# w_down of the second group in seven products over pairs of steps, with the weight sums made beside the projection

## The chip, the cores and the metric

The kernel runs on one core of a Trainium2 chip. What counts is the device time of one execution in microseconds. Before the change it is 2610.94 us, the median of three runs between 2605.71 and 2612.57 us. One more execution was recorded by the profiler; its own time is in the table below.

## What is computed

One layer of a hybrid decoder, for a prompt of 2048 tokens and 8 samples of 4 tokens, in float32:

```python
xn = rms_norm(x, norm_mix_pre)
qk_raw, v_m, o_m, gates, q_a, k_a, v_a = split_projection(xn @ w_in)
...                                    # mLSTM heads: y_m; sliding-window heads with sinks: y_a
mix = concatenate([y_m, y_a], axis=-1) @ w_out                 # 1024 x 1024
x = x + rms_norm(mix, norm_mix_post)
u = rms_norm(x, norm_ffn_pre)
f = square(relu(u @ w_up)) @ w_down                            # 1024 x 4096, 4096 x 1024
x = x + rms_norm(f, norm_ffn_post)
x = x + sigmoid(x @ w_pgate) * (p @ w_pproj)
```

The outputs are x for the prompt and the samples, and the states of both kinds of heads.

## The kernel before

**Precision.** Each float32 matrix is split into a high part, rounded to the type that TensorE multiplies at full rate, and a low part, the rest. `mm3` makes a product of three matmuls (high by high, high by low, low by high), so every product below counts three matmuls at line 148.

**Stages.** The prompt is 16 blocks of 128 tokens, in six chunks of three or two blocks. First the projection runs over all six chunks (`project`), with the mLSTM, the attention and the decoding of the samples beside it. Then three groups of two chunks follow (blocks 0 to 5, 6 to 11, 12 to 15 with the samples): w_out, the MLP and the gate. In the names of the trace `mo` is a result of w_out, `up` of w_up, `dn` of w_down, `pg` of the gate; `f` holds the sums of w_down and `hh`, `hl` are the parts of the squared activations.

**The MLP.** It has 16 steps of two tiles of 128 hidden columns each. Steps 0 and 1 are plain. In steps 2 to 15 w_up is done for both chunks together with seven block products in place of eight (`up_both`; the sums of the activations are made once for a group, those of the weights in the ring). w_down is plain in all steps: two halves of 512 output columns, two chunks, three blocks, two tiles and three passes, 72 matmuls a step in a group of six blocks. Each block's result stands in one of three banks of the pool `ps_mm` and VectorE adds it to `f` (L1759). w_up's results have two banks of their own (`ps_s`), added by VectorE at L1734.

**Weights.** `Ring` brings all weights in the order that `plan()` gives. A weight that comes first is loaded raw through SyncE's queue into one of five raw buffers (`RAWS`; L351, L363), copied to its high part by ScalarE (L254), and its low part is subtracted by VectorE and GpSimd in turn (L255). The two parts stand in one of seven pair buffers (`PAIRS`). A weight that is needed again is stored to DRAM as a split pair by GpSimd's queue (L282, `wk<-w` in the trace) and loaded from there the next time by SyncE's (L289, `w<-wk`).

**Order.** TensorE's instructions are pinned in the order in which the program writes them. Work beside the main line comes from generators, called sides, that are asked for their next piece between products after so many microseconds of estimated TensorE time; `pe.drain` empties one. The other engines' instructions are placed by a scheduler, except those marked with `here`, which keep their program order. Each engine works through its instructions in order, and so does each queue of DMA issues (SyncE's and GpSimd's). A buffer of a pool goes to the next tile that asks for it, and the first write into it waits until the last reader of the old tile is done.

The part of the main program where the projection ends:

```python
    for ci, blocks in enumerate(CHUNKS):
        project(ci, blocks)
    pe.drain(swa)
...
    es_proj.close()
    es0.close()
```

## Time and profile before

| | |
|---|---|
| profiled execution, its own time | 2623.78 us |
| its span in the trace | 2621.7 us |
| mean granted TensorE clock | 0.989 |
| chain that ended last: TensorE's share | 77%, of which w_up 21%, w_down 21%, w_out 5%, the gate 5% |
| w_down's matmuls, high part of the activations (`dn<-w,hh`) | 1792, 564.0 us busy |
| w_down's matmuls, low part (`dn<-w,hl`) | 896, 354.5 us busy |
| VectorE's additions of w_down's results (L1759) | 420, 286.9 us busy |
| transfers over the whole span | 651.10 MB, 248 GB/s on average |

The time of the execution is the span and some two microseconds around it. An engine's busy time is the sum of its instructions' times. Matmul records overlap, so that their busy times by group add up to more than the time on the clock; the pace of TensorE is better read from the chain, whose pieces follow each other. In the views below "x" stands for a number of instructions, "out<-in" for the tiles an instruction writes and reads, and what follows "<-" in brackets behind an idle time is what ended it.

### The profile page before, as it was taken

The page shows a single profiled execution, that of the slowest core. Times are in us where ns is not written, and L with a number is a line of the kernel's source. Part 1 is how long each engine was busy: PE and PEld are TensorE (multiplying, and loading weights), DVE is VectorE, ACT ScalarE, POOL GpSimd, SP SyncE. Part 2 cuts the span into 40 slices and gives each one's busy share as a digit, 9 for nine tenths or more (in the row PEclk, how much of TensorE's full clock was granted, in tenths as well). Part 3 has the DMA queues.
Part 4 walks back from the last instruction along what each step waited for, and adds up shares of the span by engine and source line. Part 5 has one row for each costly group of instructions (what it writes and reads, how often), then busy time and mean ns, then how long its engine had stood idle before and what let it go on. Part 6 is the DMA issues. An engine that isn't in the chain of part 4 may idle for free.

```text
span 2621.7 us, 39337 instructions
## 1 busy us (share of the span) xinstructions
PE 2534.7 (97%) x14260; PEld 2204.3 (84%) x14260; DVE 1483.0 (57%) x3162; ACT 974.3 (37%) x2167; POOL 620.3 (24%) x988
## 2 busy tenths in 40 slices
PE   7999999998999999999999999999999999999998
PEld 7787888777778888888877788999998879999986
DVE  6666656665657655656744654444446346444553
ACT  5545444544445444444523342222223134222231
POOL 5311111112433666666523200000001011000010
PEclk9999999999999999999999999999999999999999
DMA  9756656576898666666799765555556899777787
GB/s 315 273 192 201 207 181 213 194 244 227 260 343 287 254 250 253 244 254 251 271 341 318 255 201 188 188 191 188 187 187 233 295 334 359 253 255 256 256 299 235
DMA packets 220433, 651.10 MB, mean 248 GB/s; under 512 B 25397, under 2 KB 59401, under 8 KB 220224
## 3 DMA queue, kind: packets, MB, share of 16 engines
q1 hardware_dynamic: 170032, 474.02, 53.4%
q0 software_dynamic: 50160, 174.54, 17.3%
q8 instruction: 113, 1.85, 0.3%
q14 instruction: 80, 0.66, 0.1%
q10 hardware_dynamic: 48, 0.03, 0.0%
HBM read 494.34 MB, written 155.25 MB: 248 GB/s over the span
## 4 chain that ended last, share of the span: by engine, by line
PE 77%; DVE 8%; DMA 7%; issue 3%; ACT 2%; POOL 2%; SPq 0%; ACTq 0%; DVEq 0%; POOLq 0%
PE up L148 21%; PE dn L148 21%; PE mo L148 5%; PE pg L148 5%; PE v L148 3%; DMA w<-wk 3%; PE o L148 3%; DMA wk<-w 2%; PE qk L148 2%; PE qa L148 2%; PE gv L148 2%; DVE hl L232 2%; PE aT L152 1%; PE aO L148 1%; PE pv L148 1%
## 5 line engine op out<-in xcount | busy, mean ns | idle before, releaser
L148 PE MATMUL dn<-w,hh 128*128 128x512 f32 x1792 | 564.0, 396 | 6.3 <-ACT re L1654 3.8
L1759 DVE TENSOR_TENSOR f<-f,dn 128x512 f32<-128x512 f32 x420 | 286.9, 686 | 220.5 <-PE dn L148 218.4
L148 PEld LDWEIGHTS dn<-w,hh 128*128 128x128 f32 x1792 | 334.2, 189 | 84.7 <-DVE f L1759 6.8
L148 PE MATMUL dn<-w,hl 128*128 128x512 f32 x896 | 354.5, 396 | 1.6 <-DVE hl L232 1.6
L1734 DVE TENSOR_TENSOR re<-up,re 128x384 f32<-128x384 f32 (+1 forms) x294 | 151.9, 517 | 320.2 <-PE up L148 320.2
L148 PEld LDWEIGHTS dn<-w,hl 128*128 128x128 f32 x896 | 168.8, 188 | 43.5 <-DVE hl L232 5.1
L1735 ACT COPY re<-up 128x384 f32<-128x384 f32 (+1 forms) x42 | 18.8, 448 | 392.0 <-PE up L148 392.0
L1654 ACT ACTIVATE re<-re 128x384 f32<-128x384 f32 (+1 forms) x168 | 83.0, 494 | 207.5 <-DVE re L1734 203.9
L232 DVE TENSOR_TENSOR hl<-re,hh 128x384 fp32r<-128x384 f32 (+1 forms) x192 | 137.6, 717 | 16.8 <-ACT hh L231 15.7
L282 POOL DMA_DIRECT2D wk<-w x242 | 134.1, 556 | 34.4 <-DVE w L255 25.2
L254 ACT CAST w<-wr 128x512 fp32r<-128x512 f32 (+2 forms) x152 | 88.9, 597 | 95.9 <-PE up L148 32.3
L254 ACT CAST w<-wb 128x512 fp32r<-128x512 f32 x98 | 60.6, 620 | 168.4 <-PE dn L148 114.6
L255 POOL TENSOR_TENSOR w<-wr,w 128x512 fp32r<-128x512 f32 (+2 forms) x76 | 100.2, 1319 | 80.5 <-ACT w L254 79.5
L255 POOL TENSOR_TENSOR w<-wb,w 128x512 fp32r<-128x512 f32 x70 | 92.3, 1319 | 110.3 <-ACT w L254 109.8
L1460 POOL DMA_DIRECT2D x<-x1d x16 | 8.7, 545 | 463.5 <-PE up L148 449.4
L1655 ACT ACTIVATE re<-re 128x384 f32<-128x384 f32 (+1 forms) x192 | 94.9, 494 | 5.9
L231 ACT CAST hh<-re 128x384 fp32r<-128x384 f32 (+1 forms) x192 | 92.6, 482 | 8.3
L1067 ACT ACTIVATE s<-s,swt 128x257 f32<-128x257 f32 (+1 forms) x128 | 63.3, 496 | 65.8 <-DVE swt L1064 65.8
L1061 DVE CUSTOM_DVE_ANT_0 s<-aS,cst,sink 128x256 f32<-128x256 f32 (+1 forms) x128 | 57.1, 472 | 52.0 <-PE aS L148 51.6
L148 PE MATMUL up<-t2h,w 128*128 128x384 f32 (+1 forms) x336 | 85.1, 320 | 0.0
L148 PE MATMUL up<-t0h,w 128*128 128x384 f32 (+1 forms) x336 | 85.1, 320 | 0.0
L148 PE MATMUL up<-t1h,w 128*128 128x384 f32 (+1 forms) x336 | 85.1, 320 | 0.0
(1526 smaller groups left out, 6415.7 us busy)
## 6 DMA issues: line engine op xcount, KB each, us to landing
w<-wk SPq DMA_DIRECT2D x728, 512.0 KB, 4.9
wk<-w POOLq DMA_DIRECT2D x238, 512.0 KB, 7.2
wr<-in_w_down_dram SPq DMA_DIRECT2D x64, 256.0 KB, 8.2
wb<-in_w_up_dram SPq DMA_DIRECT2D x28, 512.0 KB, 6.9
w<-wk SPq DMA_DIRECT2D x20, 528.0 KB, 3.9
x<-in_x_prompt_dram SPq DMA_DIRECT2D x16, 512.0 KB, 4.4
y<-yd SPq DMA_DIRECT2D x32, 256.0 KB, 7.0
xr<-in_x_prompt_dram POOLq DMA_DIRECT2D x16, 512.0 KB, 9.4
```

The source lines that it names most:

```text
L148: ins = self.pe.matmul(out, lhsT, rhs, start=start, stop=stop)
L231: act.copy(hi, src)
L232: dve.tensor_tensor(lo, src, hi.bitcast(F32), ALU.subtract)
L254: act.copy(hi, src)
L255: ins = (eng or weng()).tensor_tensor(lo, src, hi.bitcast(F32), ALU.subtract)
L282: here(put(self.kept[key], t.bitcast(U32)))
L1061: dve.tensor_tensor_reduce(s_[:, s, lo : 2 * P], pS[:, s, lo:], bias[:, j, lo:], 1.0 if s == 0 else 0.0625, sink[:, h : h + 1], ALU.add, A ...
L1067: act.activation(e_, e_, AF.Exp, bias=nm[:, s : s + 1], accum_out=sm[:, s : s + 1])
L1654: act.activation(t, src, AF.Relu)
L1655: act.square(t, t)
L1734: add = lambda out, a, b: dve.tensor_tensor(out, a, b, ALU.add)
L1759: dve.tensor_tensor(out(i), out(i), ps, ALU.add)
```

## The change

In steps 2 to 13 of the second group (`SEVEN`, `SGROUP`) w_down is done over pairs of steps with seven block products instead of eight. Rows of the two by two scheme are the two chunks, its columns the two hidden tiles of a step, and the columns of the result are the two halves of w_down's output. Both steps of a pair are accumulated in the same bank.

- `up_seven` takes the place of `up_both`: it makes the four blocks of activations and four sums of them, s1 to s4, and splits each (`parts`), on VectorE (L1754 and L1723 of the kernel after the change) and GpSimd.
- `down_seven` does the seven products of a pair in the order A12, A11, s3, A22, s1, s4, s2. Three of them go to two sums each; two products go to a common sum U, which `share` adds to nine blocks on GpSimd after step 13. The gain of the last norm, `gffn`, is loaded after that, since U takes its buffer.
- The sums of w_down's blocks, four of them for each of the twelve steps, are made beside the projection by the new side `prep`, from the second chunk on (`differences`): four loads by GpSimd's queue into raw buffers of the ring, four subtractions on VectorE, four stores to DRAM by GpSimd's queue. They are emptied out (`pe.drain(prep)`) at the projection's end. `Ring.diff` loads such a sum later like a raw weight and splits it with GpSimd.
- `rows_seven` puts the weights of a pair in the plan in the order of the products.
- The pool `sp2` has one buffer instead of two, and the pool `wide` is closed in the second group before step 2, where `hq`, `wq` and `us` take its place.

```diff
+SEVEN = range(2, STEPS - 2)
+SGROUP = 1
+DIFW = 16.0, 4.0, 8.0
...
-    swa, mls, tsp = pe.side(), pe.side(), pe.side()
+    swa, mls, tsp, prep = [pe.side() for _ in range(4)]
...
+        def diff(self, key, src):
+            def make(h, l):
+                raw = self.load(512)
+                dma(raw, src)
+                wsplit(h, l, raw, pool)
+            return self.get(key, 512, make)
...
+        def diff(s, i):
+            return ("t", s, i), lambda key: ring.diff(key, td[s, i])
+        def rows_seven(steps):
+            for i, k, half in ((0, 1, 0), (0, 0, 0), (3, 0, 0), (4, 0, 0), (1, 0, 0), (0, 1, 1), (2, 0, 0)):
+                for s in steps:
+                    yield diff(s, i) if i else row(w_down, s * FS + k, half)
...
             for s in range(FAST, STEPS):
...
-                yield from rows_down(s)
+                if gi == SGROUP and s in SEVEN:
+                    if s % 2:
+                        yield from rows_seven((s - 1, s))
+                else:
+                    yield from rows_down(s)
...
+    td = {(s, i): dram.tile([P, 512], F32, name=f"td{s}{i}") for s in SEVEN for i in range(1, 5)}
     ring.set_plan(plan())
+    def differences():
+        sub = lambda out, a, b: here(dve.tensor_tensor(out, a, b, ALU.subtract))
+        for s in SEVEN:
+            b11, b21, b12, b22 = b = [ring.load(512) for _ in range(4)]
+            for n, t in enumerate(b):
+                k = s * FS + n % 2
+                here(put(t, w_down[k * P : (k + 1) * P, n // 2 * 512 : n // 2 * 512 + 512]))
+            yield DIFW[0]
+            for i, out, x, y in ((1, b11, b12, b11), (3, b12, b22, b12), (2, b22, b22, b11), (4, b21, b21, b22)):
+                sub(out, x, y)
+                yield DIFW[1]
+            for i, out in ((1, b11), (3, b12), (2, b22), (4, b21)):
+                here(put(td[s, i], out))
+            yield DIFW[2]
...
     for ci, blocks in enumerate(CHUNKS):
+        if ci == 1:
+            prep.add(differences())
         project(ci, blocks)
     pe.drain(swa)
+    pe.drain(prep)
...
-    sp2 = es2.enter_context(tc.tile_pool(name="sp2", bufs=2, reuse_waits="tile"))
+    sp2 = es2.enter_context(tc.tile_pool(name="sp2", bufs=1, reuse_waits="tile"))
...
-        gffn = gain(A["norm_ffn_post"], f"gffn{gi}")
...
+        if gi != SGROUP:
+            gffn = gain(A["norm_ffn_post"], f"gffn{gi}")
...
+        def rectify(t):
+            act.activation(t, t, AF.Relu)
+            act.square(t, t)
+        def two_tiles(pool_, nm):
+            return [pool_.tile([P, UW], F32R, tag=f"h{e}", name=f"h{e}{nm}") for e in "hl"]
+        def parts(pool_, t, nm, eng, to=None):
+            h, l = [y[:, : t.shape[1]] for y in to or two_tiles(pool_, nm)]
+            act.copy(h, t)
+            eng.tensor_tensor(l, t, h.bitcast(F32), ALU.subtract)
+            return h, l
+        def up_seven(s, X, hq, wq):
+            W = X[0][0].shape[2]
+            nm = f"{G}{s}"
+            product = products(s, X)
+            A = {}
+            t = [wp.tile([P, UW], F32, tag="re", name=f"re{nm}{n}")[:, :W] for n in range(4)]
+            s1 = wq.tile([P, UW], F32, tag="s1", name=f"s1{nm}")[:, :W]
+            add = lambda out, a, b: dve.tensor_tensor(out, a, b, ALU.add)
+            act.copy(t[0], product(1))
+            add(t[1], product(2), t[0])
+            rectify(t[1])
+            a12, a11 = two_tiles(hp, f"{nm}a12"), two_tiles(hp, f"{nm}a11")
+            A["11"] = parts(hp, t[1], f"{nm}a11", dve, a11)
+            add(t[0], product(6), t[0])
+            add(t[2], product(7), t[0])
+            add(t[3], product(4), t[2])
+            rectify(t[3])
+            A["12"] = parts(hp, t[3], f"{nm}a12", dve, a12)
+            ps = product(5)
+            add(t[2], ps, t[2])
+            add(t[0], ps, t[0])
+            rectify(t[2])
+            A["22"] = parts(hp, t[2], f"{nm}a22", dve)
+            add(t[0], product(3), t[0])
+            rectify(t[0])
+            pool.tensor_tensor(s1, t[0], t[2], ALU.add)
+            dve.tensor_tensor(t[0], t[1], t[0], ALU.subtract)
+            A["s3"] = parts(hq, t[0], f"{nm}s3", dve)
+            A["s1"] = parts(hq, s1, f"{nm}s1", pool)
+            pool.tensor_tensor(t[1], s1, t[1], ALU.subtract)
+            pool.tensor_tensor(t[3], t[3], t[1], ALU.subtract)
+            A["s4"] = parts(hp if s % 2 else hq, t[3], f"{nm}s4", pool)
+            A["s2"] = parts(hp if s % 2 else hq, t[1], f"{nm}s2", pool)
+            return A
+        def down_seven(s, As, U, first):
+            c0, c1 = chunks
+            def out(ci, half):
+                return lambda i: f[chunks[ci][i]][:, half * 512 : half * 512 + 512]
+            u = lambda i: U[i]
+            uses = (
+                ("12", out(0, 0)),
+                ("11", u, out(0, 0)),
+                ("s3", out(1, 1), out(1, 0)),
+                ("22", out(1, 0)),
+                ("s1", out(1, 1), out(0, 1)),
+                ("s4", out(0, 1)),
+                ("s2", u),
+            )
+            for n, (a, *to) in enumerate(uses):
+                w = [[t[:, :512] for t in w] for w in ring.take(2)]
+                for i in range(len(c0)):
+                    ps = psum(ps_mm, f"ds{G}{s}{n}{i}")
+                    for e in range(2):
+                        mm3(ps, [y[:, cols(i)] for y in As[e][a]], w[e], e == 0, e == 1)
+                        pe.tick()
+                    for m, o in enumerate(to):
+                        if first and n == 1 and m == 0:
+                            act.copy(o(i), ps)
+                        else:
+                            dve.tensor_tensor(o(i), o(i), ps, ALU.add)
+        def share(U):
+            for ci, half in ((0, 1), (1, 0), (1, 1)):
+                for i, b in enumerate(chunks[ci]):
+                    v = f[b][:, half * 512 : half * 512 + 512]
+                    pool.tensor_tensor(v, v, U[i], ALU.add)
+        def products(s, X):
...
+            return product
...
-            turn = iter(X)
...
+            product = products(s, X)
...
-                ring.wide = es_t.enter_context(tc.tile_pool(name="wide", bufs=WIDE, side="right", reuse_waits="tile"))
+                es_w = ExitStack()
+                ring.wide = es_w.enter_context(tc.tile_pool(name="wide", bufs=WIDE, side="right", reuse_waits="tile"))
...
         for s in range(FAST, STEPS):
+            if gi == SGROUP and s in SEVEN:
+                if s == SEVEN[0]:
+                    es_w.close()
+                    es_w = ExitStack()
+                    side = lambda nm, n: es_w.enter_context(tc.tile_pool(name=nm, bufs=n, side="right", reuse_waits="tile"))
+                    hq, wq = side("hq", 5), side("wq", 1)
+                    U = gp.tile([P, 2, 512], F32, tag="g", name=f"us{G}")
+                    U = [U[:, 0], U[:, 1], side("us", 1).tile([P, 512], F32, name=f"ut{G}")]
+                    As = []
+                As.append(up_seven(s, X, hq, wq))
+                if len(As) == 2:
+                    down_seven(s, As, U, s == SEVEN[1])
+                    As = []
+                if s == SEVEN[-1]:
+                    share(U)
+                    gffn = gain(A["norm_ffn_post"], f"gffn{gi}")
+                continue
...
+                es_w.close()
...
```

Three places show how the instructions are moved. The first is SyncE's queue near the end of the projection. In the kernel before, these rows stand among the last raw loads of w_in: `wr217` to `wr221` are the raw tiles of the first five w_out weights, and `w37` to `w40` are stored pairs of w_in for the second chunk.

```order
L351 DMA wr36_1474<-in_w_in_dram 128x512 [waits DMAHW7_49,DVE_49]
L351 DMA wr217_7677<-in_w_out_dram 128x512 [waits DMAHW6_49,Pool_49]
L351 DMA wr218_7683<-in_w_out_dram 128x512 [waits DMAHW0_49,Pool_49]
L351 DMA wr219_7752<-in_w_out_dram 128x512 [waits DMAHW1_49,DVE_49]
L351 DMA wr220_7759<-in_w_out_dram 128x512 [waits DMAHW3_49,DVE_49]
L289 DMA w37_1497<-wk0_193 128x1056 [waits DMASW3_49,DMASW6_49,DMASW0_49,PE_49]
L289 DMA w38_1500<-wk1_200 128x1056 [waits DMASW4_49,DMASW1_49,PE_49]
...
L363 DMA wr221_7799<-in_w_out_dram 64x512 [waits DMAHW4_49,Pool_49]
L289 DMA w40_1505<-wk3_216 128x1056 [waits DMASW7_49,DMASW4_49,DMAHW5_49,DMASW2_49,PE_49]
```

In the changed kernel SyncE's rows of the same tiles stand behind the last loads of the attention's and the samples' outputs (`y_5`, from `yd51`), at the end of the projection:

```order
L889 DMA y_5_8025<-yd51_161 128x512 [waits DMAHW2_49,DMASW6_49]
L354 DMA wr217_8001<-in_w_out_dram 128x512 [waits DMASW5_49,DMASW4_49,DMAHW3_49,DMASW0_49,DVE_49]
L354 DMA wr218_8007<-in_w_out_dram 128x512 [waits DMAHW4_49,DMAHW3_49,Pool_49]
L354 DMA wr219_8045<-in_w_out_dram 128x512 [waits DMAHW5_49,DMAHW4_49,DVE_49]
L354 DMA wr220_8052<-in_w_out_dram 128x512 [waits DMAHW6_49,DMAHW5_49,Pool_49]
L366 DMA wr221_8083<-in_w_out_dram 64x512 [waits DMAHW7_49,DMAHW6_49,DVE_49]
L366 DMA wr221_8083<-in_w_out_dram 64x512 [waits DMAHW0_49]
L366 DMA wr222_8091<-in_w_out_dram 64x512 [waits DMASW6_49,DMASW5_49,DMAHW1_49,DMASW2_49,DMASW1_49]
L366 DMA wr222_8091<-in_w_out_dram 64x512 [waits DMAHW2_49]
L366 DMA wr223_8117<-in_w_out_dram 64x512 [waits DMASW3_49,DMASW1_49]
```

The raw loads of w_out have moved from the start of the second chunk to the end of the projection, and each of `wr218` to `wr221` now waits for the engine that splits the tile ahead of it (VectorE or GpSimd) and for that tile's own load; `wr222` and `wr223` wait for transfers of GpSimd's queue (DMASW).

The second place is VectorE's queue behind w_up of step 5 of the second group, the odd step of a pair. `re150` to `re153` are that step's four blocks of activations, `ds15ni` is the result of product n (0 to 6) of the pair for block i, and `us1` and `ut1` hold the common sum:

```order
L1734 TENSOR_TENSOR re150_16915<-up153_17035,re150_16915 128x384 [waits DVE_49,PE_49]
L1792 TENSOR_TENSOR f6_14489<-f6_14489,ds1500_17077 128x512 [waits PE_49]
L1754 TENSOR_TENSOR re150_16915<-re151_16916,re150_16915 128x384 [waits Pool_49]
L1792 TENSOR_TENSOR f7_14490<-f7_14490,ds1501_17085 128x512 [waits PE_49]
L1723 TENSOR_TENSOR hl15s3_17056<-re150_16915,hh15s3_17055 128x384 [waits Activation_49]
L1723 TENSOR_TENSOR hl15a22_17032<-re152_16917,hh15a22_17031 128x384 [waits PE_49,Activation_49]
L1792 TENSOR_TENSOR f8_14491<-f8_14491,ds1502_17093 128x512 [waits PE_49]
L1792 TENSOR_TENSOR us1_16207<-us1_16207,ds1510_17105 128x512 [waits PE_49]
L1792 TENSOR_TENSOR f6_14489<-f6_14489,ds1510_17105 128x512
L1792 TENSOR_TENSOR us1_16207<-us1_16207,ds1511_17114 128x512 [waits PE_49]
L1792 TENSOR_TENSOR f7_14490<-f7_14490,ds1511_17114 128x512 [waits DVE_49]
L1792 TENSOR_TENSOR ut1_16211<-ut1_16211,ds1512_17123 128x512 [waits PE_49]
```

The results of product 1 (`ds1510` to `ds1512`) are added twice, once to each of their two sums, as are those of products 2 and 4 further on, and the subtraction and the splits of the activation sums (L1754, L1723) stand between the first additions. Before, one addition for each result stood there (L1759), and no sums of activations.

The third place is SyncE's queue behind the last pair, where the gain of the last norm is loaded (`gffn1`); `w711` to `w715` are stored pairs of w_up and w_down for step 14.

```order
L292 DMA w710_19552<-wk203_13060 128x1024 [waits DMAHW6_49,DMAHW1_49,PE_49]
L292 DMA w711_19568<-wk204_13075 128x1024 [waits DMAHW7_49,DMAHW2_49,PE_49]
L292 DMA w712_19590<-wk205_13100 128x1024 [waits DMAHW0_49,PE_49,Pool_49]
L1497 DMA gffn1_19491<-in_norm_ffn_post_dram 128x1024 [waits DVE_49,Pool_49]
L292 DMA w713_19613<-wk206_13128 128x1024 [waits PE_49,Activation_49]
L292 DMA w714_19634<-wk207_13154 128x1024 [waits DMAHW3_49,PE_49]
L292 DMA w715_19636<-wk208_13161 128x1024 [waits DMAHW4_49,PE_49]
```

Before, the gain was loaded at the start of the group's MLP. Now its load stands in front of `w713` and waits for VectorE and for GpSimd, which adds the common sum.

15 lines of the change are left out of this document (8 added, 7 removed).

## The prediction

> **What bounds the kernel now.** I read the page's busy shares first, then the busy time by stretches of the program, then the chain of work that ended last, and last the single rows at the places where the change puts something.
>
> ```profile
> span 2621.7 us, 39337 instructions
> ...
> PE 2534.7 (97%) x14260; PEld 2204.3 (84%) x14260; DVE 1483.0 (57%) x3162; ACT 974.3 (37%) x2167; POOL 620.3 (24%) x988
> ```
> ```profile
> core 0: us, PE busy (x) PEld busy (x) DVE busy (x) ACT busy (x) POOL busy (x), PEclk, DMA share, GB/s
> ...
> 260.00:360.00 100.00, 98.23 (x646) 84.83 (x645) 62.89 (x199) 46.49 (x125) 12.26 (x33) 1.00 0.60 196
> ...
> 680.00:770.00 90.00, 82.08 (x379) 64.36 (x378) 56.37 (x114) 40.59 (x93) 33.60 (x48) 0.94 0.86 296
> ...
> 1576.00:1952.00 376.00, 376.00 (x1873) 338.36 (x1872) 169.76 (x279) 81.56 (x157) 0.00 (x0) 1.00 0.56 185
> ```
>
> TensorE is the bound nearly everywhere, and most plainly in the stretch the change is about: from 1576 to 1952 us it is busy in all 376.00 of 376 us, with VectorE at 45%, ScalarE at 22% and GpSimd at nothing. So whatever TensorE is spared there is gained at once, until another engine fills up. Where TensorE does wait, at 680 to 770 us, the kernel leaves the input projection and begins with w_out. Both places count below.
>
> **The products that go.** The chain shows one step of the second group: 84 matmuls of w_up, then 72 of w_down, without a pause.
>
> ```profile
> 1575.53 14.74 PE up L148 x84
> 1590.27 16.80 PE dn L148 x72
> ...
> 1700.99 14.73 PE up L148 x84
> ```
>
> From 1575.53 to 1700.99 are four steps: 31.37 us a step. Less 14.73 for w_up that leaves 16.64 us for 72 matmuls, 0.231 us each. Two steps now have 2 x 72 = 144 of them, and with seven products 7 x 3 blocks x 2 steps x 3 passes = 126. Six pairs of steps save 6 x 18 = 108 matmuls, 108 x 0.231 = **25.0 us**. Nothing waits on these steps but the next ones, so if no other engine fills up, all of it is gained.
>
> **What the other engines get in those steps.**
>
> ```profile
> L1759 DVE TENSOR_TENSOR f<-f,dn 128x512 f32<-128x512 f32 x145 | 99.8, 688 | 88.4 <-PE dn L148 88.4
> ...
> L232 DVE TENSOR_TENSOR hl<-re,hh 128x384 fp32r<-128x384 f32 x48 | 26.5, 551 | 2.1 <-ACT hh L231 2.0
> ```
> ```profile
> L1759 DVE TENSOR_TENSOR f<-f,dn 128x512 f32<-128x512 f32 x153 | 103.8, 684 | 69.4 <-PE dn L148 68.2
> L232 DVE TENSOR_TENSOR hl<-re,hh 128x384 fp32r<-128x384 f32 x48 | 57.4, 1195 | 0.3 <-ACT hh L231 0.2
> ```
> ```profile
> L255 POOL TENSOR_TENSOR w<-wb,w 128x512 fp32r<-128x512 f32 x59 | 77.7, 1317 | 99.7 <-ACT w L254 99.2
> ```
>
> The first pair of rows is from 1576 to 1952 us, the other two fences from 900 to 1330 us, the same steps in the first group, where GpSimd is busy. Over a pair of steps all is well: VectorE adds 30 blocks of 0.69 us instead of 24 (+4.1), and five operations of 0.55 us a step on top (+5.5), 39 us of some 58; GpSimd has eight weight subtractions of 1.3 us and twelve smaller ones, about 23 us. But three of the seven products go to two sums each. Such a product's block takes TensorE 6 x 0.231 = 1.39 us and VectorE 2 x 0.688 = 1.38 us, with three result banks between them, and the second and third product stand next to each other. In the first 12.5 us of a pair VectorE has 15 such adds (10.3 us) and four other operations that partly wait for GpSimd's sum s1: 2.2 us at 0.55 each, so 12.5 in all. It is just full there. With three bank times of slack I get no stall at 551 ns, and about 1.3 us a pair if three of the four operations take 1195. I take half a microsecond a pair, **+3 us**, nearer the free row because GpSimd works in only two fifths of the time; the bounds are 0 and 8, and for a stall at each of the six two-sum blocks in front 15.
>
> The Trainium skill (SBUF — State Buffer, Who interferes with whom) says that a VectorE instruction with two SBUF inputs and a GpSimd instruction that reads SBUF shut each other out, while one with a single SBUF input does not collide. The trace agrees: the split with two SBUF inputs goes from 551 to 1195 ns, the add out of PSUM stays at 688 and 684. By that rule, with every such operation hit, this term would be 8 instead of 3.
>
> **The junction of projection and w_out.** This is the dearest part. The block sums go through four of the five raw weight buffers all through the projection. Before, these buffers took the first w_out rows early and held them; now the rows of SyncE show w217 to w221, the first five w_out tiles, taking one and the same buffer in turn, each load waiting for the split of the tile ahead, and w222, w223 waiting for the stores of the last sums. ScalarE's rows show w217's cast behind the last cast of x6h.
>
> ```profile
> 666.93 1.13 ACT L254 CAST w<-wr 128x512 fp32r<-128x512 f32 x2
> ...
> 685.80 0.62 ACT L239 CAST x6h<-g 128x512 fp32r<-128x512 f32 x1 [0.68 <-DVE g L238]
> ```
> ```profile
> 680.57 0.62 PE L148 MATMUL mo<-w,x6h 128*128 128x512 f32 x2
> ...
> 703.08 0.73 PE L148 MATMUL mo<-w,x6h 128*128 128x512 f32 x2 [0.81 <-DVE f L1571]
> ...
> 726.92 1.19 PE L148 MATMUL mo<-w,yt01h 128*128 128x512 f32 x2 [3.73 <-DVE ms L1490]
> ...
> 732.96 0.62 PE L148 MATMUL mo<-w,yt01h 128*128 128x512 f32 x2
> ...
> 741.54 0.73 PE L148 MATMUL mo<-w,yt01h 128*128 128x512 f32 x2 [1.99 <-DMA w<-wk]
> ...
> 769.25 0.35 PE L148 MATMUL up<-ut00h,w 128*128 128x384 f32 x1
> ```
> ```profile
> L254 ACT CAST w<-wr x17: 603/620/625, 666.9 to 757.0; 128x512 fp32r<-128x512 f32 x17
> ...
> L255 POOL TENSOR_TENSOR w<-wr,w x9: 1274/1292/1870, 667.6 to 757.7; 128x512 fp32r<-128x512 f32 x9
> L255 DVE TENSOR_TENSOR w<-wr,w x8: 670/683/1381, 668.1 to 716.2; 128x512 fp32r<-128x512 f32 x8
> ...
> DMA to landing us min/median/max: 2.9/5.3/6.9
> ```
> ```profile
> wr<-in_w_out_dram SPq DMA_DIRECT2D x14, 128.0 KB, 5.9
> ...
> wr<-in_w_out_dram SPq DMA_DIRECT2D x4, 256.0 KB, 4.6
> ...
> yd<-ya POOLq DMA_DIRECT2D x2, 256.0 KB, 6.0
> ```
>
> Today the casts begin at 666.93 and w_out's first product at 680.57. Then: the last x6h cast ends at 686.4, a little sooner without the splits that stood between, say 685.5; w217 is cast by 686.1 and split by GpSimd (1.29) at 687.4. A turn of the one buffer is a landing of 4.6, a cast of 0.62 and a split of 0.68 (VectorE) or 1.29 (GpSimd), 5.9 or 6.5 us: w218 at 693.3, w219 at 699.8, w220 at 705.7. Behind that split VectorE's queue has the last mLSTM block's output, and GpSimd's the store of the last sums: issued at 708, landed (6.0) at 714, then w222's two loads (0.6 + 5.9), cast and split by 721.8. Of the eight tiles' 72 matmuls 33 are left then, 7.6 us, and 2 us for the clock: after the pause of 3.73 us in front of 726.92 three matmuls took 1.28 us, from 728.34 to 729.62, and at 732.96 0.69. So the second half begins at 731.4 instead of 703.08, **28 us late**. The last mLSTM block's products, now all ahead of w_out, run inside this time.
>
> ```profile
> 720.00:740.00 20.00, 15.82 (x63) 12.02 (x61) 9.72 (x21) 6.48 (x14) 6.51 (x12) 0.83 1.03 411
> ```
>
> Part comes back. From 703.08 to 769.25 today are 66.2 us, for 216 matmuls (49.9) and some 4.4 us of transposes: 11.9 us are pauses and half clock, because loads of weights and stores crowd there (411 GB/s from 720 to 740 us, the transfer engines all busy, the granted clock 0.83). With w_out late, the loads of the next chunk are no longer held up behind raw loads; I give back 9. Net **+19 us**. Bounds: the six transfers in the chain at 2.9 us each take off 13, and all 11.9 come back, 28 - 13 - 12 = 3; at 6.9 each and nothing given back it is 28 + 9 = 37.
>
> The Trainium skill (TensorE: Matmul & The Clock Gate, Part 1) has the array at half clock after an idle window of about 3.4 us until it was busy for as long; the trace agrees at 726.92. By its rule, charged at every one of some five such pauses, the junction would cost about 6 more; I charge the one behind the last pause, since the others are followed by waiting anyway.
>
> **The sums beside the projection.**
>
> ```profile
> L962 DVE TENSOR_TENSOR Wt<-Wt,cst 128x512 f32<-128x512 f32 x13 | 8.7, 684 | 0.0
> ```
> ```profile
> L282 POOL DMA_DIRECT2D wk<-w x145 | 80.1, 554 | 18.0 <-DVE w L255 15.5 <-issue 2.4
> ```
>
> VectorE gets 48 subtractions of 0.68 us, 33 us in about 520, where it is busy 63% and TensorE 98% (260 to 360 us). GpSimd gets 96 issues of 0.55 us, 53 us, on 12%. Some loads stand right behind the stores that free their buffers, so GpSimd's queue stands still up to 6 us, with the sink column and the mLSTM's root behind it. The cover is VectorE's idle third; without it 33 us would be lost, with it nothing. I take **+4 us**.
>
> **Behind the last pair.**
>
> ```profile
> w<-wk SPq DMA_DIRECT2D x728, 512.0 KB, 4.9
> ```
>
> GpSimd adds the common sum to nine blocks, 9 x 1.3 = 11.7 us from about 2 us before the pair's end. The gain's load waits for that and stands on SyncE's queue ahead of w713, the seventh w_up tile of step 14: issued at +10.1, landed at +15.0, wanted after six products at 12.6. **+2.5 us**; bounds 0 and 7.
>
> **Sum.** -25.0 + 19 + 3 + 4 + 2.5 = +3.5 us. The profiled execution took 2623.8 us (2621.7 and 2.1 around it) and would take 2627; it lies 12.8 above the median of the three runs shown, 2610.9, which is the scale here: **2614 us**.
>
> **Rivals.** *The junction is cheap*: landings near 3 us and the later pauses gone, junction 5 instead of 19 and the three small terms 6 instead of 9.5: -25 + 5 + 6 = -14, 2597. For it: fewer transfers crowd there. Against: six of them in a row, median 5.3. *The junction is dear*: one raw buffer in turn, landings near 6.9 us, nothing given back: 28 + 6 = 34, with the small terms -25 + 34 + 9.5 = +18.5, 2629. It is slower by more than 0.3% (7.8 us, about what a measurement of this kernel tells from no change) once the junction costs over 23. For it: the transfers just behind it ran at 411 GB/s before; against: the crowd thins. *The seven products gain nothing*: VectorE or the chain of split sums holds each pair up by 4.2 us, 25 instead of 3 in that term: 2636. Against: three banks of slack, and VectorE at two thirds.
>
> **Chances.** Forecast 0.40, cheap junction 0.28, dear junction 0.27, no gain 0.05. So faster 0.28, the same 0.40, slower 0.32. The forecast's own range is 2604 to 2619; the range for 8 in 10 reaches to the cheap case at its end, 2597, and past the dear one to that without a gain, 2638.
>
> **What will show it.** Right: w_down's matmuls 108 fewer; a pair of steps at 58.6 us plus less than a microsecond of pauses; w_out's first products from about 687 on with pauses of 5 to 9 us, w225 near 731; the first w_up matmul of the first group near 788. Wrong: a short junction, the projection's end later than 690, or pauses on VectorE's adds in each pair.

## The result and the profile after

The changed kernel takes 2622.93 us (median of six runs, 2621.88 to 2631.5), the kernel before 2610.86 us (2605.71 to 2613.69): the ratio is 1.0056, with a 95% interval from 1.0039 to 1.0074. It is slower by some 12 us. The forecast was 2614 us in a range of 2597 to 2638; the time lies in the range, but above the forecast's own range (2604 to 2619), between the forecast and the dear junction (2629).

The page of the changed kernel, its first lines (span, then busy time by engine):

```profile
span 2621.4 us, 39879 instructions
...
PE 2516.1 (96%) x14152; PEld 2185.3 (83%) x14152; DVE 1543.8 (59%) x3255; ACT 1019.1 (39%) x2254; POOL 818.1 (31%) x1213
```

The same three stretches as before the change, by engine:

```profile
260.00:360.00 100.00, 98.30 (x651) 85.64 (x650) 69.35 (x215) 44.89 (x119) 23.08 (x52) 1.00 0.72 246
680.00:770.00 90.00, 66.40 (x286) 51.39 (x283) 50.06 (x101) 33.79 (x75) 34.75 (x51) 0.81 0.81 263
1576.00:1952.00 376.00, 375.41 (x1866) 337.17 (x1865) 222.75 (x351) 135.94 (x261) 140.23 (x122) 1.00 0.65 213
```

From 680 to 770 us TensorE is busy for 66 us instead of 82, at a granted clock of 0.81. In the pairs it is as full as it was in the steps (375.4 of 376 us), with 53 us more on VectorE and 140 on GpSimd. TensorE's matmuls are 108 fewer than the 14260 before, as forecast. So the seven products work; the loss stands earlier. The chain of one pair and of the step behind the last one:

```profile
1892.77 29.50 PE up L151 x168
...
1927.29 1.37 DVE hl113a L1723
1928.66 0.61 DVE f L1792
1929.27 0.04 issue
1929.31 22.51 PE ds L151 x96
1951.82 14.73 PE up L151 x84
1966.55 16.66 PE dn L151 x72
1983.22 6.83 PE up L151 x39
```

The last pair goes from 1892.77 to 1951.82, 59.05 us (predicted 58.6 and less than one of pauses), and step 14 follows without a pause. The 126 matmuls of the pair's w_down take 29.55 us of it, 0.4 more than at 0.231 us each: at 1929.31 the chain comes to TensorE from an addition of VectorE's, and the other pairs are as long.

Step by step at the junction, TensorE's timeline in the changed kernel (what is in brackets is the idle time ahead of the row):

```profile
680.37 0.44 PE L155 MATMUL mK<-ident,qks 128*128 128x128 f32 x2
687.04 1.53 PE L151 MATMUL mS<-qks,qks 64*128 64x128 f32 x8 [6.23 <-DVE m14f L986]
...
696.45 1.22 PE L151 MATMUL mo<-w,x6h 128*128 128x512 f32 x2
...
714.57 0.80 PE L151 MATMUL mo<-w,x6h 128*128 128x512 f32 x1 [8.70 <-ACT w L257]
...
719.21 1.52 PE L151 MATMUL mo<-w,x6h 128*128 128x512 f32 x2 [2.06 <-ACT w L257]
...
729.99 0.63 PE L151 MATMUL mo<-w,x6h 128*128 128x512 f32 x2
...
738.68 0.69 PE L155 MATMUL yt5t<-ident,y 128*128 128x128 f32 x4 [2.07 <-DVE g L241]
...
790.26 0.34 PE L151 MATMUL up<-ut00h,w 128*128 128x384 f32 x1
```

The row at 729.99 is the first product of w_out's second half, 72 matmuls behind 696.45. The first four w_out tiles come without a pause, and the fifth 8.70 us late. ScalarE's timeline shows its cast waiting for the raw load, which SyncE had issued at 702.34:

```profile
713.90 0.62 ACT L257 CAST w<-wr 128x512 fp32r<-128x512 f32 x1 [8.79 <-DMA wr<-in_w_out_dram]
```

GpSimd's timeline shows the rest. The last stores of sums (`td`) stand behind the states' outputs, and only their landing frees the raw buffers of the sixth tile and the next ones; the chain that ended last runs through that landing.

```profile
703.86 0.58 POOL L1015 DMA_DIRECT2D yd<-ym  x1 [0.69 <-DVE ym L991]
704.44 1.61 POOL L507 DMA_DIRECT2D td<-wr  x3
711.18 0.54 POOL L507 DMA_DIRECT2D td<-wr  x1 [5.13 <-DMA out_dram<-C]
```
```profile
704.44 10.36 DMA td<-wr
...
718.17 5.22 DMA wr<-in_w_out_dram
```

### The profile page after: what moved, and what is told of

Same layout as the page of the kernel before. It is cut to its first block, busy times and chain, and to the rows that moved or that the text cites. A ratio compares the mean times of both kernels' runs of the same rounds, so it can differ in the third digit from the quotient of the medians.

```text
span 2621.4 us, 39879 instructions
## 1 busy us (share of the span) xinstructions
PE 2516.1 (96%) x14152; PEld 2185.3 (83%) x14152; DVE 1543.8 (59%) x3255; ACT 1019.1 (39%) x2254; POOL 818.1 (31%) x1213
## 4 chain that ended last, share of the span: by engine, by line
PE 60%; DVE 5%; DMA 4%; issue 2%; POOL 2%; ACT 1%; SPq 0%; DVEq 0%; ACTq 0%; POOLq 0%
PE up L151 21%; PE dn L151 14%; PE pg L151 6%; PE mo L151 5%; PE ds L151 5%; DMA w<-wk 2%; PE pv L151 2%; DVE hl L235 2%; DMA wk<-w 1%; POOL w L258 1%; DVE re L1872 1%; DMA wr<-in_w_out_dram 1%; ACT w L257 0%; DMA td<-wr 0%; DMA wb<-in_w_up_dram 0%
## 5 line engine op out<-in xcount | busy, mean ns | idle before, releaser
L151 PE MATMUL dn<-w,hh 128*128 128x512 f32 x1216 | 384.1, 397 | 6.1 <-ACT re L1699 3.5
L151 PEld LDWEIGHTS dn<-w,hh 128*128 128x128 f32 x1216 | 225.6, 188 | 61.1 <-DVE f L1897 7.4
L1897 DVE TENSOR_TENSOR f<-f,dn 128x512 f32<-128x512 f32 x276 | 188.1, 686 | 132.7 <-PE dn L151 130.3
L151 PE MATMUL dn<-w,hl 128*128 128x512 f32 x608 | 241.1, 397 | 1.2 <-DVE hl L235 1.2
L1872 DVE TENSOR_TENSOR re<-up,re 128x384 f32<-128x384 f32 (+1 forms) x210 | 105.2, 501 | 201.8 <-PE up L151 201.8
L258 POOL TENSOR_TENSOR w<-wr,w 128x512 fp32r<-128x512 f32 (+2 forms) x124 | 163.8, 1321 | 121.4 <-ACT w L257 120.5
L151 PEld LDWEIGHTS dn<-w,hl 128*128 128x128 f32 x608 | 114.6, 188 | 31.0 <-DVE hl L235 4.9
L235 DVE TENSOR_TENSOR hl<-re,hh 128x384 fp32r<-128x384 f32 (+1 forms) x144 | 112.6, 782 | 13.3 <-ACT hh L234 12.2
L1792 DVE TENSOR_TENSOR f<-f,ds 128x512 f32<-128x512 f32 x144 | 94.1, 683 | 30.0 <-PE ds L151 26.1
L1699 ACT ACTIVATE re<-re 128x384 f32<-128x384 f32 (+1 forms) x120 | 57.8, 482 | 112.0 <-DVE re L1872 108.4
L258 DVE TENSOR_TENSOR w<-wr,w 128x512 fp32r<-128x512 f32 (+2 forms) x76 | 61.0, 809 | 53.9 <-ACT w L257 51.9
```

The source lines that it names most:

```text
L151: ins = self.pe.matmul(out, lhsT, rhs, start=start, stop=stop)
L235: dve.tensor_tensor(lo, src, hi.bitcast(F32), ALU.subtract)
L258: ins = (eng or weng()).tensor_tensor(lo, src, hi.bitcast(F32), ALU.subtract)
L1699: act.activation(t, src, AF.Relu)
L1792: dve.tensor_tensor(o(i), o(i), ps, ALU.add)
L1872: add = lambda out, a, b: dve.tensor_tensor(out, a, b, ALU.add)
```

## The experiments

All runs below were compared with runs of the kernel before on the same chip, and each left one profile. "The control" is the kernel before, once more. A mark is that of one execution: of the profiled ones the control's took 5 us less than the median of its kernel, e1's 7 and e7's 8 more, and the one shown before the change 13 more, so that a few microseconds between two rows are not told apart. The table has the marks that they are read by: the start of the last low-part product of the projection's `o`, the first w_up product, the stretch from the first gate product of the first group to the second group's first w_out product, the mean length of a pair of steps in the second group, and the ratio to the kernel before.

| kernel | projection's end | first w_up | gate | pair | ratio (95%) |
|---|---|---|---|---|---|
| before, the profile shown | 679.9 | 769.3 | 88.0 | 62.7 | 1 |
| before, once more | 672.4 | 757.2 | 88.2 | 62.7 | 0.9993 (0.9982 to 1.0003) |
| the change | 679.0 | 790.3 | 90.8 | 59.1 | 1.0056 (1.0039 to 1.0074) |
| e1, sums made, not used | 685.2 | 793.3 | 88.2 | 62.8 | 1.0109 (1.0096 to 1.0122) |
| e2, seven products, no sums made | 672.1 | 759.5 | 91.2 | 59.0 | 0.9932 (0.9919 to 0.9944) |
| e7, ten steps | 690.0 | 778.7 | 91.2 | 59.0 | 1.0008 (0.9995 to 1.0021) |
| e4, pace 13 | 692.4 | 781.2 | 93.3 | 59.0 | 1.0006 (0.9994 to 1.0018) |
| e3, pace 10 | 690.8 | 779.2 | 91.9 | 59.0 | 0.9988 (0.9978 to 0.9998) |
| e5, pace 10, no subtractions | 685.8 | 771.2 | 91.5 | 59.0 | 0.9966 (0.9954 to 0.9978) |
| e9, pace 10, on GpSimd | 704.2 | 793.7 | 90.7 | 59.0 | 1.0037 (1.0022 to 1.0053) |
| e6, sums made in the first group | 673.9 | 759.4 | 90.9 | 59.0 | 1.0060 (1.0041 to 1.0078) |
| e8, sums made in the pairs | 670.3 | 755.4 | 95.9 | 67.9 | 1.0181 (1.0158 to 1.0204) |
| e10, three pairs | 678.5 | 766.1 | 92.2 | 60.2 | 0.9993 (0.9983 to 1.0004) |
| e11, two parts | 683.3 | 771.3 | 87.7 | 60.2, first 68, last 63 | 1.0070 (1.0054 to 1.0086) |

**The kernel before, once more.** No edit.

> The kernel before, unchanged, once more: for a second profile, since the profiled execution shown lies 12.8 us above the median, and the two profiles (2621.7 and 2621.4 us) show no difference where the medians show 12. Theory A: the profiled execution lost these 12 us before the end of the projection, in stalls of chunks 0, 1 and 5 where transfers crowd; then w_out starts some 8 to 12 us earlier here (near 670 instead of 680.6) and the first w_up matmul near 758 instead of 769.3, with the steps of the second group at 31.37 us as before. Rival B: the time is lost evenly or behind 770 us; then the marks at 680 and 769 stay within 2 us and a later stage is shorter. Time: ratio to the kernel before within 0.3% of 1.

Theory A holds for the most part: of the 18.8 us between the two spans 7.5 lie before the projection's end and 4.6 between there and w_up. The row of the first group's w_up products, which gives their first and last start, in the profile shown and in this one:

```profile
L148 PE MATMUL up<-ut00h,w x288: 331/336/421, 769.3 to 1265.9; 128*128 128x384 f32 x144
L148 PE MATMUL up<-ut00h,w x288: 331/336/421, 757.2 to 1252.7; 128*128 128x384 f32 x144
```

It starts at 757.2 instead of 769.25; the span is 2602.9. Five microseconds more lie between there and the second group. So the profile the prediction was made on held pauses that the execution need not have, and a stage can only be compared across several profiles. In the five kernels without sums beside the projection (two of before, e2, e6, e8) w_up starts at 755.4 to 769.3, 760.2 on average.

**e1 and e2: one half of the change each.** In e1 `SGROUP` names no group, so that the differences are made and w_down stays plain:

```diff
-SGROUP = 1
+SGROUP = -1
```

> The differences of w_down's blocks are made beside the projection and stored, but nobody uses them: w_down of the second group is plain as before. Theory: the seven products gain 22 us (six pairs at 59.06 instead of 62.7), so without them the time is 2623 + 22 = 2645, ratio 1.013 to before; all of the loss (34 us) stands before the first w_up matmul, 21 of it at the junction. Rival: the seven products gain the full 25 and the trace's 0.5 us a pair is made up elsewhere: 2648. Rival: the junction's loss is given back later: 2630 or less.

e2 leaves out the block sums of w_down and takes single blocks in their place:

```diff
-            return ("t", s, i), lambda key: ring.diff(key, td[s, i])
+            k = s * FS + i % 2
+            src = w_down[k * P : (k + 1) * P, i // 3 * 512 : i // 3 * 512 + 512]
+            return ("t", s, i), lambda key: ring.diff(key, src)
...
-        if ci == 1:
-            prep.add(differences())
```

> The seven products without the preparation: no differences are made, and the weights that should be sums are loaded raw from single blocks of w_down, so the values of the second group are not the reference's; every instruction of the pairs stays. Theory: the w_out rows are loaded early as before, the junction costs nothing, and the pairs save 22 us: 2611 - 22 = 2589, ratio 0.9916. Rival: the pairs' gain is partly lost behind the last pair or in raw loads: 2592 to 2600.

e1 costs 1.09%, 28 us, where 34 were expected; e2 gains 0.68%, 18 us, where 22 were, so that for e2 the rival holds. Together they make 10.7 us, and the change 14.6 by its ratio (10 to 19): the two halves add up. e2's pairs save 22.4 us (353.9 for all six, in the control 376.3), so some 4 us of that are lost elsewhere in it; 3 of them are in the gate's stretch, below. e1's row of w_up's start says where its loss is: the first product comes 33 us behind the average of the five (in an execution 7 us above e1's median), and nothing is lost behind it.

```profile
L151 PE MATMUL up<-ut00h,w x288: 334/336/423, 793.3 to 1290.1; 128*128 128x384 f32 x144
```

**e3, e4 and e7: the preparation ends earlier.** e3 and e4 change only the pace, e7 only the number of steps:

```diff
-DIFW = 16.0, 4.0, 8.0
+DIFW = 10.0, 2.5, 5.0
...
-SEVEN = range(2, STEPS - 2)
+SEVEN = range(2, STEPS - 4)
```

(the first pair of lines is e3, with 13.0, 3.5, 6.5 in e4; the second pair is e7)

> The preparation is paced faster (10, 2.5 and 5 us between its pieces instead of 16, 4 and 8), so that it ends one and a half chunks before the projection does and the w_out tiles get the raw buffers early again. Theory: the junction is as before and only the preparation's own cost in the projection (about 12 us, its traffic and VectorE's subtractions) stays: 2623 - 21 = 2602, ratio to before 0.9965. Rival: the preparation's cost comes from VectorE and grows when it is packed closer: 2610 to 2620. Rival: it costs nothing but the junction: 2590.

> The preparation at an intermediate pace (13, 3.5 and 6.5 us), ending about half a chunk before the projection. Measured so far: at the pace of the change (16, 4, 8) the projection ends 6.6 us later than in the control and the junction costs 22 to 26; at 10, 2.5, 5 the projection ends 18.3 later and the junction costs nothing. Theory: the projection's cost grows with the density of the preparation, so here some 11 us and no junction: 2612 + 11 - 20 = 2603, ratio 0.9965. Rival: the projection's cost is one sum per piece whatever the pace, and the 18 were the early raw loads of w_out in SyncE's queue: then this is like the faster pace, 2609.

> Steps 2 to 11 instead of 2 to 13 (five pairs), the pace of the change kept, so that the preparation is as dense as in the change but ends some 80 us earlier, ahead of the projection's end. Theory: the junction costs nothing, the projection 6 us, five pairs save 18: 2612 + 6 - 18 = 2600, ratio 0.9955. Rival (the junction's cost is not from the raw buffers held until the projection's end, but from w_out beginning beside the outputs of the states or from the earlier place of the last mLSTM block): the junction stays 20 us late: 2620.

In all three the junction, from the projection's end to the first w_up product, is short again: 88.4, 88.8 and 88.7 us, against 111.3 in the change and 108.1 in e1, and 84.8 to 89.4 in the kernels without a preparation (the table's second column less its first). So the junction's loss does come from the raw buffers that the last sums hold. But the projection ends later, at 690 to 692 instead of 679 (685 in e1), and half of the gain is gone. All three theories had the time too short, e3's by 6 us, e4's by 11 and e7's by 14, since they took the projection's cost too low; e4's rival, that it would be like the faster pace, is nearer. e7, as dense as the change, shows that density alone is not it: its first chunk with sums costs what the change's does (124.8 and 124.7 us from one chunk's start to the next, against 116.3 without sums), and it loses in the last two chunks, 196.5 us against 188.0 in the change and 189.4 in the control. What takes them there was not tried. The raw loads of w_out are issued in them, but those cannot be all of it: e1, in which they stand as late as in the change, has 194.4 us there.

**e5 and e9: what the subtractions cost.** e5 leaves the subtractions out, so that the sums of the second group are single blocks; e9 gives them to GpSimd. Both are otherwise e3.

```diff
-        sub = lambda out, a, b: here(dve.tensor_tensor(out, a, b, ALU.subtract))
+        sub = lambda out, a, b: here(pool.tensor_tensor(out, a, b, ALU.subtract))
```

(e9; in e5 the line `sub(out, x, y)` is gone)

> The fast pace (10, 2.5, 5) with the 48 subtractions on VectorE left out; loads and stores stay, and what is stored are the blocks themselves, so the sums of w_down are left out of the second group. Theory A: the preparation costs the projection time through the transfers (its loads and stores delay the weight pairs and outputs that the projection waits for): the projection's end stays near +18 and the time within 5 us of 2609. Theory B: it costs through VectorE, whose queue the mLSTM's chain waits in: the projection's end goes back to within 6 us of the control and the time to about 2596. Both in part: 2600 to 2605.

> The fast pace (10, 2.5, 5) with the 48 subtractions on GpSimd instead of VectorE. Measured: 0.9988 with them on VectorE, 0.9966 without them. Theory A (they cost through VectorE's queue, in which the mLSTM's chain stands): as without them, 0.997, the projection's end near 685. Rival B (a GpSimd operation holds VectorE up as well, and the preparation's stores and the outputs wait behind it in GpSimd's queue): 0.9988 or more, the projection's end at 690 or later.

Without them the projection ends 5 us sooner and the time is 0.22% less: both in part, as the third case had it. Better counted is the stretch from the second chunk's start, since the first chunk, to which nothing is added, takes 121 to 128 us from profile to profile. From there to the projection's end are 537.1 us on average in the five kernels, 554.9 in e3 and 546.1 in e5: of e3's 17.8 us about half are the subtractions, and half is what stays in e5, the transfers and their issues. On GpSimd, which is busy an eighth of the time from 260 to 360 us in the kernel before and a quarter in e3, they cost more than three times as much (0.71% above e5, the end at 704.2), and rival B holds. GpSimd takes 1.30 us for one, and VectorE's instructions that read two tiles in SBUF slow down meanwhile. The convolution's rows from 250 to 480 us, in the control, in e3 and in e9:

```profile
L772 DVE SCALAR_TENSOR_TENSOR acc<-u,pcol,acc 128x384 f32<-128x384 f32 x24 | 14.8, 618 | 0.6
```

```profile
L813 DVE SCALAR_TENSOR_TENSOR acc<-u,pcol,acc 128x384 f32<-128x384 f32 x24 | 14.8, 618 | 0.6
```

```profile
L813 DVE SCALAR_TENSOR_TENSOR acc<-u,pcol,acc 128x384 f32<-128x384 f32 x24 | 18.7, 780 | 0.6
```

The same 24 instructions take 780 ns instead of 618, and not yet in e3, from which e9 differs by the engine of the subtractions alone. That two such instructions shut each other out is what the Trainium skill says (SBUF — State Buffer, Who interferes with whom), and the trace agrees. How much of the 13 us between e3 and e9 is that, and how much GpSimd's queue, which the subtractions hold for 62 us and in which outputs and loads are issued, was not told apart.

**e6: the sums from the first group's own raw blocks.** The four raw w_down blocks of a step are in the raw buffers in the first group anyway; they are subtracted there, two weights later.

```diff
+        def differ(self):
+            while self.due and self.due[0][0] + DIFL <= self.n:
+                _, s, (b11, b21, b12, b22) = self.due.pop(0)
+                for out, x, y in ((b11, b12, b11), (b12, b22, b12), (b22, b22, b11), (b21, b21, b22)):
+                    dve.tensor_tensor(out, x, y, ALU.subtract)
+                for i, out in ((1, b11), (3, b12), (2, b22), (4, b21)):
+                    here(put(td[s, i], out))
...
```

> The differences are made in the first group's MLP from the four raw w_down blocks that each step loads there anyway: no loads of their own, the subtractions two weights later, the stores as before; nothing is added to the projection. Theory: projection and junction as in the kernel before; in the first group VectorE (62% busy) and the transfers (67%) have room, so that at most 5 us are lost there; the pairs save 22: 2612 - 22 + 3 = 2593, ratio 0.993. Rival: the raw buffers are held until the stores land, the loads of w_down wait for them in SyncE's queue, and the w_up blocks behind them come late, 1 to 2 us in each of twelve steps: 2605 to 2615.

Projection and junction are those of the kernel before, and the first group's MLP loses 37 us (569.6 us from its first w_up product to the gate's first, against 532.6 in the control): the wait is VectorE's, not SyncE's as the rival had it. VectorE's rows from 900 to 1240 us, the control and e6:

```profile
L255 DVE TENSOR_TENSOR w<-wb,w 128x512 fp32r<-128x512 f32 x22 | 15.1, 684 | 1.3 <-ACT w L254 0.3
```

```profile
L258 DVE TENSOR_TENSOR w<-wb,w 128x512 fp32r<-128x512 f32 x20 | 31.4, 1568 | 0.0
L397 DVE TENSOR_TENSOR wr<-wr,wr 128x512 f32<-128x512 f32 x40 | 27.4, 686 | 11.8 <-POOL w L258 11.8
```

The subtractions take their 686 ns, but the splits of w_up's blocks take 1568 ns instead of 684, as if they now ran beside GpSimd's work, and the subtractions stand 11.8 us waiting for GpSimd's split, with all of VectorE's queue behind them. TensorE's waits in the same stretch (us in total, times, longest), the control and e6:

```profile
PE dn L148 <- DVE f L1759: 2.3, 9, 0.3
```

```profile
PE up L151 <- DVE re L1880: 16.4, 10, 1.7
PE dn L151 <- DVE f L1905: 11.3, 8, 2.5
```

TensorE waits for VectorE's additions of both products, though VectorE is busy only 61% of the stretch in the control and 66% in e6: what counts is when its queue stands still, not its share.

**e8: the sums made in the pairs.** Three raw blocks a step are loaded while w_up runs, the fourth when a buffer comes free; no DRAM copy.

```diff
+        def fetch(steps, dq):
+            for n, s in enumerate(steps):
+                for m, i in ((0, 1), (2, 3), (3, 2)):
+                    t = td[s, i] = dq(n + i)
+                    put(t, block(s, m))
+        def differences(steps):
+            for s in steps:
+                t1, t3, t2 = [td[s, i] for i in (1, 3, 2)]
+                dve.tensor_tensor(t1, t3, t1, ALU.subtract)
+                dve.tensor_tensor(t3, t2, t3, ALU.subtract)
+                dve.tensor_tensor(t2, t2, t1, ALU.subtract)
...
```

> The block sums are made inside the second group itself, a pair of steps at a time: three raw blocks a step are loaded by GpSimd's queue while w_up runs, six subtractions on VectorE and two on GpSimd for a pair, and the sums are split where they stand. No preparation beside the projection, no stores to DRAM, no raw loads of sums in SyncE's queue. Theory (the change lost by where the sums were made, not by the seven products): projection and junction as before, the pairs save 22 less up to 1 us a pair for the sums, and the 3 us of the first group's gate, where the first raw loads of sums stood ahead of the gate's weights in SyncE's queue, come back: 2612 - 18 = 2594, ratio 0.993, pairs at 59 to 60 us, from the gate's first product to the second group's w_out 88 us instead of 91. Rival: the fourth sum waits for a raw buffer that the first ones hold, and its load (5 to 7 us) delays the fourth product: pairs at 62 us or more, 2610.

The rival is right that the pairs get longer, but 67.9 us and a time of 2660 are far beyond its 62 and 2610, and the wait is another one. VectorE's timeline of e8 in the second pair:

```profile
1694.39 3.05 DVE L1761 TENSOR_TENSOR wr<-wr,wr 128x512 f32<-128x512 f32 x1 [5.16 <-DMA wr<-in_w_down_dram]
1697.37 3.07 DVE L1794 TENSOR_TENSOR f<-f,ds 128x512 f32<-128x512 f32 x5
```

A subtraction of the next pair waits 5.16 us for its load and takes 3.05, and five additions of results stand behind it; TensorE then waits for a result bank, 38.0 us in the six pairs:

```profile
PE ds L150 <- DVE f L1794: 38.0, 15, 7.2
```

The last pair, behind which no next one is prepared, takes 62.2 us, the others 65.5 to 71.7. Six buffers for the eight blocks of a pair make the next pair's loads wait, and so its subtractions, in a queue that runs in order.

**e10 and e11: the sums where they seemed free.** Both start with the third chunk and load the sums through GpSimd's queue; e10 does three pairs, e11 six, with the second half of the sums beside the second group's w_out.

```diff
-                dma(raw, src)
+                put(raw, src)
                 wsplit(h, l, raw, pool)
...
-        if ci == 1:
-            prep.add(differences())
+        if ci == 2:
+            prep.add(differences(range(2, 8), 1.0))
...
             if gi == 1:
                 dec.add(decode())
+                prep.add(differences(range(8, 14), 0.8))
```

(e11; in e10 there is one call, with all of its steps, 2 to 7)

> Three pairs only (steps 2 to 7), their sums made beside chunks 2 and 3, where the preparation at the change's pace (16, 4, 8) cost nothing in three profiles (both chunks as long as without it, within 1 us; chunk 1 was 5 to 8 longer), and the raw loads of sums put on GpSimd's queue, so that they no longer stand ahead of the gate's weights on SyncE's. Theory: no junction, projection within 2 us, the gate's stretch 88 us instead of 91, three pairs save 11: 2612 - 11 + 2 = 2603, ratio 0.9965. Rival: the preparation costs wherever it stands, about 1 us a step, and the gate's 3 us stay: 2610.

> All six pairs; the sums of steps 2 to 7 are made beside chunks 2 and 3 as in the kernel with three pairs, those of steps 8 to 13 beside the second group's w_out and its two plain steps at 0.8 of the pace, where VectorE is busy 51%. Theory: the pairs save 22, the first part costs 1 to 2, the second up to 6, since the transfers are busy 80% there: 2612 - 22 + 6 = 2596, ratio 0.994. Rival: the weight pairs of w_out and of the plain steps come late behind the preparation's loads and stores, so that the stretch from the second group's first w_out product to its first pair grows by 15 us or more: 2606 or later.

e10 is as fast as the kernel before; its pairs are 1.2 us longer, by one wait of 1.1 to 1.2 us for VectorE's addition in each. The chain that ended last comes to that addition through GpSimd, where the issue of a sum's load (0.56 us) stands ahead of the activation sum. e10's rival holds. e11 is slower: from the second group's first w_out product to its first pair are 199 us instead of the control's 181, and w_up waits 6 us in its first pair. Its rival has the time right and the reason wrong, since TensorE hardly waits for weight pairs there:

```profile
PE dpd L151 <- DVE dec L1251: 13.4, 1, 13.4
...
PE mo L151 <- DMA w<-wk: 0.7, 2, 0.5
```

One product of the samples' decoding waits 13.4 us for VectorE, in the control 2.0, and the chain that ended last runs there through a store of sums that takes 10.00 us to land. So the preparation cost time in every place where it was tried.

The gate's stretch has an answer here that the theory had missed. It is 87.7 to 88.2 us in the four kernels in which no sum or block for the first pair is loaded then, and 90.7 to 95.9 in all others, also in e8 and e10, where those loads are not in SyncE's queue. So it is not the place in that queue alone. In the change these are five blocks of 256 KB:

```profile
1354.43 2.40 SPq L374 DMA_DIRECT2D wr<-td  x3
...
1362.61 0.80 SPq L374 DMA_DIRECT2D wr<-td  x2
```

The whole stretch by engine, in the control and in the change:

```profile
1289.80:1378.00 88.20, 84.89 (x387) 68.11 (x386) 41.11 (x66) 21.30 (x39) 21.39 (x32) 1.00 0.94 347
```

```profile
1323.80:1414.60 90.80, 87.28 (x387) 70.36 (x386) 40.44 (x66) 21.17 (x38) 21.47 (x32) 0.97 0.95 348
```

The transfer engines are as full in the one as in the other; 1.31 MB more at 348 GB/s take 3.8 us, by which later loads can be late (an estimate). TensorE idles 3.5 us in the change and 3.3 in the control, but at one time, waiting for a stored weight pair, where the control's longest wait is 1.7; behind it the granted clock falls, and of the 2.6 us that are lost 2.4 are matmuls that take longer. That the five loads cause the longer wait is argued from these rows and was not tried alone. In e8 the longest wait of the stretch, 6.1 us, is put down to ScalarE's result of the gate and not to a weight.

Of the kernels that make and use all twelve steps' sums, only e3 is ahead of the kernel before, by 0.12%, and its interval (0.9978 to 0.9998) all but reaches 1.

## Why the prediction came out as it did

Compared are the changed kernel's profile and the kernels without sums beside the projection.

- **The products that go, 25.0 less 3 of pauses: right.** Six pairs take 354.4 us instead of the control's 376.3, 21.9 less, so that half a microsecond a pair is lost, as taken, and at the place that was named: once a pair, near its front, TensorE waits some 0.4 us for VectorE's additions. Otherwise the three result banks hide the two additions of a block. The 39 us of VectorE's work in a pair should have been 38 by its own terms; 35 were measured.
- **The junction, +19: the mechanism right, the net too small, and the step that failed is the 9 us given back.** The second half of w_out was forecast at 731.4 and starts at 729.99; counted from the projection's end that is 51.0 us, in the control 22.9, so 28.1 late where 28 was forecast. The control's row:

```profile
695.32 0.73 PE L148 MATMUL mo<-w,x6h 128*128 128x512 f32 x2 [0.81 <-DVE f L1571]
```

One part of the way was different: the first product was at 696.45 and not at 687, since the last mLSTM block's products stand ahead of it and wait 6.23 us on VectorE; it cost nothing in the end, because the fifth tile's load and the stores set the end. That the 28 came out so well is in part luck. The one buffer's turns were 4.6 to 6.4 us and not 5.9 to 6.5, so that the first of the last stores was issued at 704.44 and not at 708; but it took 10.36 us to land, not 6.0, and a load behind it took 3.07 instead of 5.9. But from 729.99 to w_up are 60.3 us, against 66.2 in the profile shown and 61.9 in the control: 1.6 to 6 us come back, not 9. Of the 11.9 us of pauses 4.3 were this one profile's, since the control has them no more, and 6.0 are still there in the changed kernel. The junction is 111.3 us from the projection's end, against 86.4 on average without a preparation: **+24.9**. e3, e4 and e7 show that it goes when the last sums are stored earlier.
- **The sums beside the projection, +4: too small.** The projection ends at 679.0 in the change and 685.2 in e1, against 673.7 on average in the five others: 5 to 11, and 8 to 11 from the second chunk's start. The idle third of VectorE covered most of the 33 us of subtractions. The transfers were given no price of their own, and at the faster pace e5 shows that they and their issues cost about as much as the subtractions.
- **Behind the last pair, +2.5: wrong, nothing.** The load of the gain waits only for the six additions that read its buffer, not for nine, and is issued at 1957.38, 5.6 us behind the pair's end instead of 10.1:

```profile
1957.38 0.33 SPq L1497 DMA_DIRECT2D gffn<-in_norm_ffn_post_dram  x1
```

- **Not foreseen, +2.7:** the gate's stretch, in which the raw loads of the first pair's sums now stand.

Sum: -21.9 + 24.9 + 5.3 + 2.7 = +11.0, and +13.3 with the 7.6 us of the projection from the second chunk's start, +17 with e1's projection; measured 12 by the medians and 14.6 by the ratio. The forecast was 9 us too low, and its sign of a slower kernel, a junction over 23, is what happened. The forecast of +3.5 counted the pauses of one execution as time that would come back. The dear junction, 2629, gave nothing back, which is nearer to what came, but it missed by 6 us, since it added another 6 for slow landings all along the way: slow were only the fifth tile's load and the last stores, and others were faster than taken.

## What to carry to other kernels

A saving on the engine that bounds is real when its own stage is full, as it was here to within half a microsecond a pair; what makes it possible has to be paid at the place where it is made, and "idle a third of the time" is an average that says little about the moments when a queue is full. Before a buffer is lent to a side task, look at who takes it next and when, and let the task end earlier than that. A pause in one profile is no reserve: profile the unchanged kernel twice before something is counted as coming back.

## What the hardware showed that was not expected

- Moving 48 subtractions from VectorE to a GpSimd that was busy a quarter of the time made them dearer: the projection's end went from 690.8 to 704.2, and VectorE's convolution instructions from 618 to 780 ns.
- Pauses of two microseconds were enough for the lower clock. After one of 2.07 us in the changed kernel, the first wait since 719.21, the rows of two matmuls take 1.13 and 1.05 us instead of 0.62, for four microseconds, and the granted clock is 0.50 from 740 to 742 us. In the control the same follows on a pause of 2.60 us:

```profile
739.09 1.13 PE L151 MATMUL mo<-w,x6h 128*128 128x512 f32 x2
740.02 0.63 PE L151 MATMUL mo<-w,x6l 128*128 128x512 f32 x1
740.45 1.05 PE L151 MATMUL mo<-w,x6h 128*128 128x512 f32 x2
...
742.83 0.63 PE L151 MATMUL mo<-w,x6h 128*128 128x512 f32 x2
```
```profile
717.99 1.19 PE L148 MATMUL mo<-w,yt01h 128*128 128x512 f32 x2 [2.60 <-DMA w<-wk]
718.98 0.63 PE L148 MATMUL mo<-w,yt01l 128*128 128x512 f32 x1
719.41 1.06 PE L148 MATMUL mo<-w,yt01h 128*128 128x512 f32 x2
```

The Trainium skill (TensorE: Matmul & The Clock Gate, Part 1) gives an idle window of about 3.4 us for this; here 2.07 and 2.60 us did it. A pause of 1.15 us in the control, ahead of 699.70, did not.
- A stretch in which the transfers ran at 348 GB/s became 2.6 us longer when 1.31 MB were loaded in it that nobody needed for another 270 us. TensorE idled no longer in all; one wait grew from 1.7 to 3.5 us, and most of the loss was the lower clock behind it.
